# Long convolutions: one kind of PSUM bank for all steps, and filter columns loaded one at a time

## The chip, the cores and the metric

The kernel runs on one core of a Trainium2 chip. The metric is the device time of one execution in microseconds (us). A core has a matrix engine (TensorE, PE in the rows; its weight loads are PEld), a vector engine (VectorE, DVE), an activation engine (ScalarE, ACT), a general-purpose engine (GpSimd, POOL) and a sync engine (SyncE, SP) whose queue issues most of the transfers here. Each engine takes its instructions in order. Matmul results land in PSUM, which has eight banks of 128 partitions by 512 float32 each.

## The reference, cut to what matters

An encoder layer runs over two requests, of 256 and 2048 tokens. One projection of the normalised input feeds two mixers: gated long convolutions over 512 channels, and dilated window attention with 8 heads. Both results are normalised, concatenated, projected and added to the input; a gated feed-forward part follows. The mixer that the change touches:

```python
def long_conv(z, kf, skip):
    L = z.shape[1]
    zf = z.astype(jnp.float32)
    y = jnp.fft.irfft(jnp.fft.rfft(zf, n=2 * L, axis=1) * kf[None], n=2 * L, axis=1)[:, :L]
    return (y + skip.astype(jnp.float32) * zf).astype(z.dtype)

def hyena_mixer(u, short_w, short_b, w1, b1, sin_freq, w2, b2, w3, decay, skip):
    ...
    z = x1 * long_conv(v, kf[:, 0], skip[0])
    z = x2 * long_conv(z, kf[:, 1], skip[1])
    return z
...
    hy = hyena_mixer(proj[..., :3 * HY_WIDTH], ...)
    at = dilated_attention(proj[..., 3 * HY_WIDTH:])
    mix = jnp.concatenate([rmsnorm(hy, hy_out_g), rmsnorm(at, attn_out_g)], axis=-1) @ w_out
```

## The kernel before

The long convolution is a Fourier transform in two factors, done with matmuls. For each request (r = 0, 1) and each of the two convolutions in a row (o = 0, 1), `hyena` runs four kinds of step, and each writes one PSUM bank (128 x 512 float32):

- hs1 (`hyena_first`, L692 and L693): the first factor. VectorE and GpSimd split the input into a high and a low part, two matmuls add up in a bank, ScalarE or VectorE copies it out, and the result `hae` goes to DRAM (`d_hA`).
- hs2k and hs2z (`hyena_second`, L723 and L727): the second factor, of the filter's columns `hk` and of the input's `hx`, with the table `htab`. VectorE scales the filter's (L725) and multiplies the two as complex numbers (L731 to L734), and GpSimd adds (L735).
- hs3 (L741): back through the second factor, one group later; ScalarE copies it to `hbe` (L744), which goes to DRAM (`d_hB`).
- hs4 (`hyena`, L778): back through the first factor, from `hD`; VectorE multiplies it by the gate `hg` (L779). For o = 0 the result goes on to hs1; for o = 1 it is stored as the mixer's result `d_hy` (L785).

There are 72 product groups (hs2k, hs2z, hs3) and 36 hs4 steps of two matmuls each, of which the long request has 64 and 32. hs2k and hs2z share a tag with two banks; hs1, hs3 and hs4 share another with one. `hk` has one buffer that holds two groups' columns, `hx` and the other 128 x 2 x 512 tiles share a ring of four, and the gates have two.

`mixers` (L1043 and on) weaves streams of work in the order in which they are written: the convolution's steps (`units`) beside the second half of the input projection (`project`, matmuls named pj), and then beside attention, by the numbers in `RATES`:

```python
    RATES = dict(p1=42, f=90, ad=36, h1=135, p2=39, h2=90, at=440)
            x = min(live, key=lambda y: (y[2] + 0.5) / y[1])
```

That order is an input to a scheduler, which then orders each engine's instructions by when it reckons that operands and buffers are ready. So the order on an engine depends on how many buffers a tile has.

Attention works through 216 blocks of two heads. For each, TensorE computes scores (aS, L906 and L907), VectorE adds the bias and takes the minimum (L910) and ScalarE the exponential (L913) into `aP`, TensorE transposes this (aT, L922), VectorE or ScalarE copies it to `aPT`, and TensorE multiplies by the values (aOp, L938). The scores and the transposes have two banks each, the values' products one; with the convolution's three, all eight are in use.

After both mixers comes the output projection, in nine blocks of 256 tokens (matmuls named om, L208 to L210). Its first block is the short request; its merged rows are ready before attention ends. Every other block needs the long request's convolution (`ohy`, loaded from `d_hy` at L1124) and all three attention branches (`oO`, L1122).

Of the kernel before, what the change touches and what calls it, by code (L numbers as in the profile page):

```python
# [13 lines left out]
F32 = mybir.dt.float32  # L14
# [4 lines left out]
PSUM = bass.MemoryType.PSUM  # L19
DRAM = bass.MemoryType.DRAM  # L20

P = 128
# [3 lines left out]
C = 512  # L26
# [163 lines left out]
class Hybrid:  # L190
# [488 lines left out]
    def hyena_first(self, wp, psp, r, An, n, z):  # L679

        nc = self.nc
        f1 = self.hc[r][0]
        for k in range(2):
            S = self.ring(wp, "hS", F32R)
            for h in range(2):
                own, oth = slice(64 * h, 64 * h + 64), slice(64 - 64 * h, 128 - 64 * h)
                nc.vector.tensor_copy(S[own, h], z[own, k])
                self.sub(nc.gpsimd, S[oth, h], z[own, k], S[own, h])
            ae = self.ring(wp, "hae")
            for h in range(2):  # L690
                ps = psp.tile([P, C], F32, tag="hpt", name="hs1", bufs=1)
                nc.tensor.matmul(ps, f1[:, 0], S[:, h], start=True, stop=False)  # L692
                nc.tensor.matmul(ps, f1[:, 1], S[:, h], start=False, stop=True)  # L693
                (nc.vector.tensor_copy if h else nc.scalar.copy)(ae[:, h], ps)
            nc.sync.dma_start(out=An[n + k], in_=ae)
            yield

    def hyena_second(self, wp, psp, r, o, A, B):

        nc = self.nc  # L700
        n2c = REQ[r][1] // 64
        rnc = wp.tile([P, C], F32, tag="hrn", name="hrn", bufs=1)
        nc.sync.dma_start(out=rnc, in_=self.rnc[r][o][0].partition_broadcast(P))
        grp = "(g p) c -> p g c"
        Ag = A.rearrange("m n c -> (m n) c").rearrange(grp, p=P)
        Kg = self.fA[r][o].rearrange("m n c -> (m n) c").rearrange(grp, p=P)
        Bg = B.rearrange(grp, p=P)
        prev = None
        be = None
        for g in range(n2c + 1):  # L710
            cur = None
            if g < n2c:
                i = g % 2
                if i == 0:
                    gs = slice(g, g + 2)
                    tab = wp.tile([P, 2, 2, P], F32, tag="htab", name="htab", bufs=2)
                    nc.sync.dma_start(out=tab, in_=self.a[f"tab_{r}"][:, gs])
                    xz = self.ring(wp, "hx")
                    nc.sync.dma_start(out=xz, in_=Ag[:, gs])
                    xk = wp.tile([P, 2, C], F32, tag="hk", name="hk", bufs=1)  # L720
                    nc.sync.dma_start(out=xk, in_=Kg[:, gs])
                ps = psp.tile([P, C], F32, tag="hps", name="hs2k")
                nc.tensor.matmul(ps, tab[:, i, 0], xk[:, i], start=True, stop=True)  # L723
                K = wp.tile([P, C], F32, tag="hK", name="hK", bufs=2)
                nc.vector.tensor_tensor(out=K, in0=ps, in1=rnc, op=ALU.mult)  # L725
                ps = psp.tile([P, C], F32, tag="hps", name="hs2z")
                nc.tensor.matmul(ps, tab[:, i, 0], xz[:, i], start=True, stop=True)  # L727
                t1 = wp.tile([P, C], F32, tag="ht1", name="ht1", bufs=3)
                t2 = wp.tile([P, C], F32, tag="ht2", name="ht2", bufs=1)
                v, lo_, up = nc.vector, slice(0, 64), slice(64, 128)  # L730
                v.tensor_tensor(out=t1[lo_], in0=ps[lo_], in1=K[lo_], op=ALU.mult)  # L731
                v.tensor_tensor(out=t1[up], in0=ps[lo_], in1=K[up], op=ALU.mult)
                v.scalar_tensor_tensor(out=t2[lo_], in0=ps[up], scalar=-1.0, in1=K[up], op0=ALU.mult, op1=ALU.mult)
                v.tensor_tensor(out=t2[up], in0=ps[up], in1=K[lo_], op=ALU.mult)  # L734
                nc.gpsimd.tensor_tensor(out=t1, in0=t1, in1=t2, op=ALU.add)  # L735
                cur = (g, tab, t1)
                yield
            if prev is not None:
                g2, tb, pp = prev
                ps = psp.tile([P, C], F32, tag="hpt", name="hs3", bufs=1)  # L740
                nc.tensor.matmul(ps, tb[:, g2 % 2, 1], pp, start=True, stop=True)  # L741
                if g2 % 2 == 0:
                    be = self.ring(wp, "hbe")
                nc.scalar.copy(be[:, g2 % 2], ps)  # L744
                if g2 % 2 == 1:
                    nc.sync.dma_start(out=Bg[:, g2 - 1:g2 + 1], in_=be)
                yield
            prev = cur

    def hyena(self, wp, psp, r):  # L750

        nc = self.nc
# [15 lines left out]
        for o in range(2):  # L768
            yield from self.hyena_second(wp, psp, r, o, A[o], B[o])
            Bm = B[o].rearrange("(m h n) c -> n m h c", h=2, n=nh)  # L770
            for q0 in range(0, nh, 2):
                x = rows_in(self.tok["x2" if o else "x1"], q0, "hg")
                for k in range(2):
                    D = self.ring(wp, "hD")
                    nc.sync.dma_start(out=D, in_=Bm[q0 + k])
                    ps = psp.tile([P, C], F32, tag="hpt", name="hs4", bufs=1)
                    for h in range(2):
                        nc.tensor.matmul(ps[64 * h:64 * h + 64], gi, D[:, h], start=True, stop=True)  # L778
                    nc.vector.tensor_tensor(out=x[:, k], in0=ps, in1=x[:, k], op=ALU.mult)  # L779
                    yield  # L780
                if o == 0:
                    yield from self.hyena_first(wp, psp, r, An[1], q0, x)
                else:
                    for h, rows in enumerate(self.time_major(self.tok["hy"], r, q0)):
                        nc.sync.dma_start(out=rows, in_=x[64 * h:64 * h + 64])  # L785
# [88 lines left out]
    def attention(self, wp, psS, psT, psO, first, mq):  # L874
        nc, a = self.nc, self.a
        q1, q2 = [], []

        def scores(heads, g, i, blk, ot, bias, b):
# [2 lines left out]
            dil = DILS[b]  # L881
            off, L = REQ[r]
            ps = psS.tile([P, 2, 256], F32, tag="aS", name="aS")
            sb = wp.tile([P, 2, 256], F32, tag="aP", name="aP", bufs=3)
            for hh in range(2):
                Ql, Ks, Qh = heads[hh]
                t0 = off + res + dil * P * j
# [91 lines left out]
        for hp in range(4):  # L979
# [6 lines left out]
            for b in range(3):  # L986
# [6 lines left out]
                for g in self.attention_groups(b, (0, 1) if hp == 3 else (1, 0)):  # L993
# [3 lines left out]
                    for i, blk in enumerate(blks):  # L997
# [3 lines left out]
                        sb, n = scores(heads, g, i, blk, ot, bias, b)  # L1001
# [41 lines left out]
    def mixers(self):  # L1043
        R = self.RATES
        proj, first, atn, left, hy = (ExitStack() for _ in range(5))
        ps = self.pool(proj, "p_ps", bufs=2, space=PSUM, side="right")
        psF = self.pool(left, "f_ps", bufs=2, space=PSUM, side="left")
        hp = self.pool(proj, "p_h", side="right")
        wp = self.pool(proj, "p_w", side="right")
# [12 lines left out]
        g = self.project(hp, wp, w2, ps, range(0, 12), H)  # L1062
# [5 lines left out]
        hb = self.pool(hy, "h_c", side="left")  # L1068
        self.hyena_consts(hb)
        wh = self.pool(hy, "h_w", side="left")  # L1070
        psH = self.pool(hy, "h_ps", bufs=2, space=PSUM, side="left")

        def units():
            for r in range(2):
# [3 lines left out]
        with ExitStack() as st:  # L1078
# [8 lines left out]
            g = self.project(hp, wp, None, ps, range(12, 24))  # L1087
# [598 lines left out]
```

## Time and profile before

| | |
|---|---|
| median of three runs | 3568.52 us (3553.45 to 3568.69) |
| the profiled execution | 3565.03 us, its span 3562.9 us |
| TensorE busy | 3303.1 us, 93% of the span |
| VectorE / ScalarE / GpSimd busy | 69% / 44% / 35% |
| mean granted clock of TensorE in the record | 0.957 |
| moved by DMA | 628 MB, 176 GB/s over the span |

The profile is of one execution. Busy time of TensorE is modelled from pipelined matmuls and so can overlap: what a matmul costs in a dense stretch is the distance to the next one and not its duration. A 128 x 512 float32 matmul shows as two records. An engine's idle time is put down to what released it. In the clock row, 9 is the full 2.4 GHz.

### The profile page before, as it was taken

The page shows a single profiled execution, that of the slowest core. Times are in us where ns is not written, and L with a number is a line of the kernel's source. Part 1 is how long each engine was busy: PE and PEld are TensorE (multiplying, and loading weights), DVE is VectorE, ACT ScalarE, POOL GpSimd, SP SyncE. Part 2 cuts the span into 40 slices and gives each one's busy share as a digit, 9 for nine tenths or more (in the row PEclk, how much of TensorE's full clock was granted, in tenths as well). Part 3 has the DMA queues.
Part 4 walks back from the last instruction along what each step waited for, and adds up shares of the span by engine and source line. Part 5 has one row for each costly group of instructions (what it writes and reads, how often), then busy time and mean ns, then how long its engine had stood idle before and what let it go on. Part 6 is the DMA issues. An engine that isn't in the chain of part 4 may idle for free.

```text
span 3562.9 us, 56859 instructions
## 1 busy us (share of the span) xinstructions
PE 3303.1 (93%) x20926; PEld 3020.3 (85%) x20926; DVE 2465.5 (69%) x4254; ACT 1561.9 (44%) x2926; POOL 1255.2 (35%) x946
## 2 busy tenths in 40 slices
PE   7989899999899999996588799999899999899998
PEld 4978798889677788773388799999899999899998
DVE  7898877764576564686388666766776666567657
ACT  4577753323345565541255433333433334344433
POOL 1487751124222231222144433333634333223222
PEclk9999999999989999997699899999999999999999
DMA  6453567676756585656666632444544224466655
GB/s 240 134 179 122 154 186 240 225 223 199 202 173 194 149 235 157 187 176 195 212 188 199 198 108 106 153 154 151 218 147 150 95 94 147 155 205 217 221 179 181
DMA packets 408334, 628.02 MB, mean 176 GB/s; under 512 B 28431, under 2 KB 231439, under 8 KB 402135
## 3 DMA queue, kind: packets, MB, share of 16 engines
q1 hardware_dynamic: 354896, 593.13, 51.2%
q10 hardware_dynamic: 52072, 28.40, 2.7%
q8 instruction: 166, 2.72, 0.3%
q0 software_dynamic: 1088, 2.85, 0.2%
q14 instruction: 112, 0.92, 0.1%
HBM read 419.03 MB, written 205.25 MB: 175 GB/s over the span
## 4 chain that ended last, share of the span: by engine, by line
PE 58%; DVE 7%; DMA 7%; issue 2%; ACT 2%; SPq 1%; POOL 1%; ACTq 0%; DVEq 0%; POOLq 0%
PE w L210 8%; PE w L208 8%; PE w L209 8%; PE fd L210 4%; PE fd L209 4%; PE fd L208 4%; PE aOp L938 4%; PE aS L906 2%; PE aS L907 2%; PE aT L922 2%; PE hs2k L723 1%; PE hs2z L727 1%; PE hs L741 1%; PE pj L209 1%; PE pj L208 1%
## 5 line engine op out<-in xcount | busy, mean ns | idle before, releaser
L208 PE MATMUL w<-hh,whi 128*128 128x288 f32 (+1 forms) x2464 | 735.4, 299 | 16.3 <-ACT whi L1345 9.9
L210 PE MATMUL w<-hh,wlo 128*128 128x290 f32 (+1 forms) x2464 | 732.2, 298 | 10.7 <-POOL wlo L203 7.0
L209 PE MATMUL w<-hl,whi 128*128 128x288 f32 (+1 forms) x2464 | 735.2, 299 | 5.2 <-DVE hl L203 5.1
L208 PEld LDWEIGHTS w<-hh,whi 128*128 128x128 f32 x2464 | 470.3, 191 | 18.2 <-ACT whi L1345 10.1
L210 PEld LDWEIGHTS w<-hh,wlo 128*128 128x128 f32 x2464 | 469.4, 191 | 12.7 <-POOL wlo L203 8.0
L209 PEld LDWEIGHTS w<-hl,whi 128*128 128x128 f32 x2464 | 472.0, 192 | 6.7 <-DVE hl L203 6.6
L208 PE MATMUL pj<-hThi,wihi 128*128 128x386 f32 (+1 forms) x1152 | 402.5, 350 | 6.6 <-ACT u L629 4.1
L209 PE MATMUL pj<-hTlo,wihi 128*128 128x386 f32 (+1 forms) x1152 | 400.9, 348 | 7.8 <-DVE hTlo L203 7.8
L210 PE MATMUL pj<-hThi,wilo 128*128 128x386 f32 (+1 forms) x1152 | 397.8, 345 | 0.0
L208 PE MATMUL fd<-hh,dwh 128*128 128x288 f32 x1210 | 359.9, 297 | 12.6 <-ACT dwh L1551 12.6
L210 PE MATMUL fd<-hh,dwl 128*128 128x288 f32 x1210 | 358.8, 297 | 0.0
L209 PE MATMUL fd<-hl,dwh 128*128 128x288 f32 x1210 | 357.5, 295 | 0.0
L735 POOL TENSOR_TENSOR ht<-ht,ht 128x512 f32<-128x512 f32 x72 | 99.0, 1376 | 432.3 <-DVE ht L734 364.1
L208 PEld LDWEIGHTS fd<-hh,dwh 128*128 128x128 f32 x1210 | 229.8, 190 | 13.3 <-ACT dwh L1551 12.9
L209 PEld LDWEIGHTS pj<-hTlo,wihi 128*128 128x128 f32 x1152 | 221.8, 193 | 20.7 <-DVE hTlo L203 9.7
L938 PEld LDWEIGHTS aOp<-aV,aPT 128*128 128x128 f32 (+1 forms) x1408 | 193.9, 196 | 52.5 <-issue 20.3
L208 PEld LDWEIGHTS pj<-hThi,wihi 128*128 128x128 f32 x1152 | 221.1, 192 | 17.7 <-ACT u L629 4.4
L210 PEld LDWEIGHTS pj<-hThi,wilo 128*128 128x128 f32 x1152 | 220.9, 192 | 12.2 <-issue 8.0
L209 PEld LDWEIGHTS fd<-hl,dwh 128*128 128x128 f32 x1210 | 229.3, 190 | 0.4
L210 PEld LDWEIGHTS fd<-hh,dwl 128*128 128x128 f32 x1210 | 227.6, 188 | 0.1
L203 POOL TENSOR_TENSOR wlo<-ws,whi 128x512 fp32r<-128x512 f32 x88 | 133.4, 1516 | 235.9 <-ACT whi L1345 235.9
L910 DVE CUSTOM_DVE_ANT_0 aP<-aS,aB 128x256 f32<-128x256 f32 (+2 forms) x432 | 136.2, 355 | 115.6 <-PE aS L907 43.4
(297 smaller groups left out, 7977.3 us busy)
## 6 DMA issues: line engine op xcount, KB each, us to landing
hl<-d_G SPq DMA_DIRECT2D x154, 288.0 KB, 5.3
dwl<-d_S SPq DMA_DIRECT2D x59, 704.0 KB, 4.1
wiraw<-in_w_in SPq DMA_DIRECT2D x72, 512.0 KB, 4.6
d_G<-cv SPq DMA_DIRECT2D x42, 576.0 KB, 3.0
wraw<-in_w_gate SPq DMA_DIRECT2D x22, 1024.0 KB, 4.8
wraw<-in_w_up SPq DMA_DIRECT2D x22, 1024.0 KB, 5.6
adat<-in_ada_t SPq DMA_DIRECT2D x36, 512.0 KB, 4.6
d_fA<-fae SPq DMA_DIRECT2D x72, 256.0 KB, 3.1
```

Of the source, the lines that this page charges most:

```text
L203: eng.tensor_tensor(out=lo, in0=x, in1=hi.bitcast(F32), op=ALU.subtract)
L208: mm(out, wh, xh, start=first, stop=False, skip_group_check=more)
L209: mm(out, wh, xl, start=False, stop=False, skip_group_check=more)
L210: mm(out, wl, xh, start=False, stop=last, skip_group_check=more)
L723: nc.tensor.matmul(ps, tab[:, i, 0], xk[:, i], start=True, stop=True)
L727: nc.tensor.matmul(ps, tab[:, i, 0], xz[:, i], start=True, stop=True)
L735: nc.gpsimd.tensor_tensor(out=t1, in0=t1, in1=t2, op=ALU.add)
L906: nc.tensor.matmul(ps[:, hh, :N], qa, rhs, start=True, stop=False)
L907: nc.tensor.matmul(ps[:, hh, :N], qb, rhs, start=False, stop=True)
L910: nc.vector.tensor_tensor_reduce(out=sb[:, hh, :n], in0=ps[:, hh, v0:v0 + n], in1=bias[:, hh, b0:b0 + n], scale=1.0, scalar=3e38, op0=ALU. ...
L922: nc.tensor.transpose(pt[:cn, hh, c], sb[:, hh, c0:c0 + cn], self.ident)
L938: nc.tensor.matmul(po[:, i, hs], pe[:cn, hh, c], vt[:cn, x["v"] + c * x["vs"], hs], start=(c == 0), stop=(c == len(ch) - 1))
```

## The change

Three things change. The tags `hps` (two banks) and `hpt` (one bank) become one tag `hp` with three banks, for all steps of the convolution. The filter's columns are loaded one group at a time into three buffers of 128 x 512, and no longer two groups at a time into one buffer of 128 x 2 x 512. To make room for them, the attention's `aP` goes from three buffers to two.

```diff
--- before.py
+++ after.py
@@ -688,7 +688,7 @@
                 self.sub(nc.gpsimd, S[oth, h], z[own, k], S[own, h])
             ae = self.ring(wp, "hae")
             for h in range(2):
-                ps = psp.tile([P, C], F32, tag="hpt", name="hs1", bufs=1)
+                ps = psp.tile([P, C], F32, tag="hp", name="hs1")
                 nc.tensor.matmul(ps, f1[:, 0], S[:, h], start=True, stop=False)
                 nc.tensor.matmul(ps, f1[:, 1], S[:, h], start=False, stop=True)
                 (nc.vector.tensor_copy if h else nc.scalar.copy)(ae[:, h], ps)
@@ -717,13 +717,13 @@
                     nc.sync.dma_start(out=tab, in_=self.a[f"tab_{r}"][:, gs])
                     xz = self.ring(wp, "hx")
                     nc.sync.dma_start(out=xz, in_=Ag[:, gs])
-                    xk = wp.tile([P, 2, C], F32, tag="hk", name="hk", bufs=1)
-                    nc.sync.dma_start(out=xk, in_=Kg[:, gs])
-                ps = psp.tile([P, C], F32, tag="hps", name="hs2k")
-                nc.tensor.matmul(ps, tab[:, i, 0], xk[:, i], start=True, stop=True)
+                xk = wp.tile([P, C], F32, tag="hk", name="hk", bufs=3)
+                nc.sync.dma_start(out=xk, in_=Kg[:, g])
+                ps = psp.tile([P, C], F32, tag="hp", name="hs2k")
+                nc.tensor.matmul(ps, tab[:, i, 0], xk, start=True, stop=True)
                 K = wp.tile([P, C], F32, tag="hK", name="hK", bufs=2)
                 nc.vector.tensor_tensor(out=K, in0=ps, in1=rnc, op=ALU.mult)
-                ps = psp.tile([P, C], F32, tag="hps", name="hs2z")
+                ps = psp.tile([P, C], F32, tag="hp", name="hs2z")
                 nc.tensor.matmul(ps, tab[:, i, 0], xz[:, i], start=True, stop=True)
                 t1 = wp.tile([P, C], F32, tag="ht1", name="ht1", bufs=3)
                 t2 = wp.tile([P, C], F32, tag="ht2", name="ht2", bufs=1)
@@ -737,7 +737,7 @@
                 yield
             if prev is not None:
                 g2, tb, pp = prev
-                ps = psp.tile([P, C], F32, tag="hpt", name="hs3", bufs=1)
+                ps = psp.tile([P, C], F32, tag="hp", name="hs3")
                 nc.tensor.matmul(ps, tb[:, g2 % 2, 1], pp, start=True, stop=True)
                 if g2 % 2 == 0:
                     be = self.ring(wp, "hbe")
@@ -773,7 +773,7 @@
                 for k in range(2):
                     D = self.ring(wp, "hD")
                     nc.sync.dma_start(out=D, in_=Bm[q0 + k])
-                    ps = psp.tile([P, C], F32, tag="hpt", name="hs4", bufs=1)
+                    ps = psp.tile([P, C], F32, tag="hp", name="hs4")
                     for h in range(2):
                         nc.tensor.matmul(ps[64 * h:64 * h + 64], gi, D[:, h], start=True, stop=True)
                     nc.vector.tensor_tensor(out=x[:, k], in0=ps, in1=x[:, k], op=ALU.mult)
@@ -881,7 +881,7 @@
             dil = DILS[b]
             off, L = REQ[r]
             ps = psS.tile([P, 2, 256], F32, tag="aS", name="aS")
-            sb = wp.tile([P, 2, 256], F32, tag="aP", name="aP", bufs=3)
+            sb = wp.tile([P, 2, 256], F32, tag="aP", name="aP", bufs=2)
             for hh in range(2):
                 Ql, Ks, Qh = heads[hh]
                 t0 = off + res + dil * P * j
@@ -1068,7 +1068,7 @@
         hb = self.pool(hy, "h_c", side="left")
         self.hyena_consts(hb)
         wh = self.pool(hy, "h_w", side="left")
-        psH = self.pool(hy, "h_ps", bufs=2, space=PSUM, side="left")
+        psH = self.pool(hy, "h_ps", bufs=3, space=PSUM, side="left")
 
         def units():
             for r in range(2):
```

The instructions stay the same but for 36 more loads; their order on the engines changes. TensorE at the end of attention, before (L922 and L938 are attention, L723, L727 and L741 the convolution's products, L1174 the transposes that open the output projection):

```order
L938 MATMUL aOp<-aV,aPT 128x65 x4
L922 MATMUL aT<-ident,aP 128x128
L727 MATMUL hs2z<-hx,htab 128x512
L938 MATMUL aOp<-aV,aPT 128x65 x2
L741 MATMUL hs_12131<-ht_11943,htab 128x512
L723 MATMUL hs2k<-hk,htab 128x512
L1174 MATMUL ot<-ident,ohy 128x128 x4
L1174 MATMUL ot<-ident,oat 128x128 x4
L741 MATMUL hs_12255<-ht_12074,htab 128x512
L1174 MATMUL ot<-ident,ohy 128x128 x4
```

The same place now:

```order
L906 MATMUL aS<-Ks,Qh 128x256
L907 MATMUL aS<-Ks,Ql 128x256
L922 MATMUL aT<-ident,aP 128x128 x3
L938 MATMUL aOp<-aV,aPT 128x65 x4
L922 MATMUL aT<-ident,aP 128x128 x4
L938 MATMUL aOp<-aV,aPT 128x65 x4
L1174 MATMUL ot<-ident,ohy 128x128 x4
L1174 MATMUL ot<-ident,oat 128x128 x4
```

Before, products of the convolution stood among the last of attention and behind it; now there are none there. TensorE at the convolution's last hs4 steps (L778, in this view named hs), before:

```order
L778 MATMUL hs_14371<-hD,hgi_5119 64x512 x2
L778 MATMUL hs_14454<-hD,hgi_5119 64x512 x2
L778 MATMUL hs_14512<-hD,hgi_5119 64x512 x2
L1174 MATMUL ot<-ident,ohy 128x128 x4
L1174 MATMUL ot<-ident,oat 128x128 x4
```

And now:

```order
L922 MATMUL aT<-ident,aP 128x128 x4
L938 MATMUL aOp<-aV,aPT 128x65 x12
L778 MATMUL hs_14584<-hD,hgi_5119 64x512 x2
L922 MATMUL aT<-ident,aP 128x128
L922 MATMUL aT<-ident,aP 64x128
L906 MATMUL aS<-Ks,Qh 128x256
L907 MATMUL aS<-Ks,Ql 128x256
```

The last of them moved from right ahead of the second block's output transposes to between blocks of attention. On SyncE's queue, the convolution's last store (L785) and the load of its result (L1124), before:

```order
L763 DMA hg<-d_x_84 64x1024 x2
L785 DMA d_hy<-hg 64x1024 x4
L1124 DMA ohy<-d_hy 128x512 x2
L1122 DMA oO<-d_O_89 128x528
L1122 DMA oO<-d_O_90 128x528
```

And now, where L958 are the last stores of attention:

```order
L958 DMA d_O_91<-aO 128x3x132
L958 DMA d_O_91<-aO 128x132
L1124 DMA ohy<-d_hy 128x512
L1192 DMA mg<-in_mixg 128x1024
L1197 DMA oraw<-in_w_out 128x8x128 x2
L1122 DMA oO<-d_O_91 128x528 x2
L1124 DMA ohy<-d_hy 128x512
```

The load of `ohy` now stands behind attention's last stores, and no longer behind the convolution's.

## Rows read from the trace of the kernel before

**Rows 1.** The page: busy time, and the clock in 40 slices.
```profile
PE 3303.1 (93%) x20926; PEld 3020.3 (85%) x20926; DVE 2465.5 (69%) x4254; ACT 1561.9 (44%) x2926; POOL 1255.2 (35%) x946
...
PEclk9999999999989999997699899999999999999999
```

**Rows 2.** Stages: from:to, length, busy us of each engine (instructions), clock, DMA share, GB/s.
```profile
500.00:944.00 444.00, 415.13 (x2182) 382.78 (x2181) 281.83 (x392) 140.79 (x220) 101.25 (x61) 0.97 0.69 218
944.00:1592.80 648.80, 623.21 (x3401) 499.54 (x3400) 430.98 (x1355) 345.75 (x830) 167.82 (x128) 0.96 0.62 184
1592.80:1754.30 161.50, 96.77 (x355) 46.20 (x354) 76.41 (x123) 25.35 (x47) 27.92 (x23) 0.69 0.69 217
1754.30:1990.30 236.00, 213.40 (x1664) 207.85 (x1662) 187.94 (x381) 128.45 (x273) 98.44 (x93) 0.94 0.61 185
```

**Rows 3.** Chain that ended last, in attention: start, us, what.
```profile
1399.61 1.01 PE hs L778 x4
...
1446.10 0.86 PE hs2z L727 x2
```

**Rows 4.** Timeline behind attention: start, us, engine, line, what, idle time before it.
```profile
1697.85 0.69 DVE L779 TENSOR_TENSOR hg<-hs,hg 128x512 f32<-128x512 f32 x1 [5.47 <-DMA hg<-d_x]
...
1701.37 1.98 PE L778 MATMUL hs<-hD,hgi 128*64 128x512 f32 x4 [0.80 <-DVE hg L779]
...
1705.75 0.69 DVE L779 TENSOR_TENSOR hg<-hs,hg 128x512 f32<-128x512 f32 x1 [4.43 <-DMA hg<-d_x]
```

**Rows 5.** Waits of SyncE's queue, 944 to 1750: us in total, times, longest.
```profile
SPq L763 <- DMA d_hy<-hg: 20.8, 6, 3.8
```

**Rows 6.** 1592.8 to 1749, busy PE and PEld, of L723, L727, L741 and L778 in turn.
```profile
1592.80:1749.00 156.20, 12.11 (x20) 3.74 (x20) 0.70 0.69 217
...
1592.80:1749.00 156.20, 11.46 (x20) 3.30 (x20) 0.70 0.69 217
...
1592.80:1749.00 156.20, 14.61 (x24) 4.08 (x24) 0.70 0.69 217
...
1592.80:1749.00 156.20, 31.59 (x64) 4.76 (x64) 0.70 0.69 217
```

**Rows 7.** Timeline from the end of attention to the second output block.
```profile
1592.25 0.56 PE L938 MATMUL aOp<-aV,aPT 128*128 128x65 f32 x4
...
1600.47 0.48 PE L208 MATMUL om<-omh,ow 128*128 128x256 f32 x2
...
1745.38 0.63 ACT L1147 ACTIVATE oO<-ohy 128x512 f32<-128x512 f32 x1 [71.08 <-DMA ohy<-d_hy]
...
1754.34 1.01 PE L208 MATMUL om<-omh,ow 128*128 128x256 f32 x3
```

**Rows 8.** Instructions of `om`: ns min/median/max, first and last start.
```profile
L210 PE MATMUL om<-omh,owl x360: 277/283/562, 1636.6 to 1990.0; 128*128 128x256 f32 x180
```

**Rows 9.** Lines of PE, 944 to 1592.8: busy us, mean ns, idle before and releasers.
```profile
L906 PE MATMUL aS<-Ks,Qh 128*128 128x256 f32 (+1 forms) x432 | 188.6, 443 | 3.6 <-DVE aO L910 3.6
...
L727 PE MATMUL hs2z<-hx,htab 128*128 128x512 f32 x100 | 57.4, 658 | 7.4 <-DVE ht L734 6.8 <-DMA hx<-d_hA 0.5
L741 PE MATMUL hs<-ht,htab 128*128 128x512 f32 x99 | 55.2, 640 | 4.8 <-POOL ht L735 4.8
L723 PE MATMUL hs2k<-hk,htab 128*128 128x512 f32 x98 | 53.2, 625 | 5.4 <-DMA hk<-d_fA 3.6 <-DVE Ks L871 1.3 <-DVE hK L725 0.5
```

**Rows 10.** Instructions of `aP`: ns min/median/max, first and last start.
```profile
L910 DVE CUSTOM_DVE_ANT_0 aP<-aS,aB x432: 274/353/426, 954.9 to 1587.8; 128x256 f32<-128x256 f32 x58, 128x128 f32<-128x128 f32 x53, 128x192 f32<-128x192 f32 x33
L913 ACT ACTIVATE aP<-aP,aO x432: 384/455/524, 955.5 to 1588.3; 128x256 f32<-128x256 f32 x58, 128x128 f32<-128x128 f32 x53, 128x192 f32<-128x192 f32 x33
```

**Rows 11.** DMA issues: count, KB each, median us to landing.
```profile
hk<-d_fA SPq DMA_DIRECT2D x36, 512.0 KB, 4.2
...
hg<-d_x SPq DMA_DIRECT2D x36, 256.0 KB, 3.6
```

## The prediction

> **What bounds the kernel now.** I read the busy line and the slices first, then the granted clock by stage, then the chain of waits and the timeline where the clock is low. TensorE is busy for 93% of the span and its clock is granted in full nearly everywhere, except in two or three slices in the middle [rows 1]. Cut into stages, the picture is plain [rows 2]: the second half of the projection (500 to 944 us) and attention (944 to 1592.8) keep TensorE busy 415 of 444 and 623 of 649 us at a clock of 0.96 to 0.97; the stretch from the last attention matmul to the output projection of its second block (1592.8 to 1754.3) is 161.5 us long, TensorE is busy there for 97 us and the clock is 0.69. That stretch is the end of the long convolution standing alone. Beside one block of the output projection, it has nothing else to run, because the second block waits for `ohy`, the convolution's last result: ScalarE's first square of it comes after an idle time of 71 us that ends with that load, at 1745 [rows 7].
>
> Inside the stretch the inverse step (L778, called hs4 in the kernel) is the slowest part. Two steps form a pair, and pairs come every 7.9 us (1697.85 to 1705.75) [rows 4]. The step has one PSUM bank, so a matmul group waits until VectorE has multiplied the previous one; VectorE in turn waits 5.47 and 4.43 us for the `hg` load; the load waits for the store from the same pair of buffers, 20.8 us in six waits [rows 5]. TensorE runs at its lower level there, 1.2 GHz: four records of L778 take 1.98 us against 1.01 us in attention at 2.4 GHz [rows 3, 4].
>
> **What the change does to the order.** The change has three edits, but the larger effect is that the scheduler now lets the convolution run ahead. In the order of TensorE's instructions, 13 of the 72 hs2k matmuls stand ahead of the first attention score before, 30 after; behind the last attention matmul stood 10 hs2k, 10 hs2z, 12 hs3 and 32 hs4 matmuls, and now none does. The trace shows the same count for the tail: 20, 20, 24 and 64 records, two for a matmul [rows 6]. The last hs4 group now stands 29 blocks of attention before its end. The sum is therefore about a serial stretch that goes, and work that reappears where TensorE is already the bound.
>
> **The sum**, against the profiled execution (3565.0 us; its span is 3562.9). It is 3.5 us under the median of the runs shown, less than these differ among themselves (3553 to 3569), so I make no correction.
>
> 1. Removed: the whole stretch, 161.5 us [rows 2].
> 2. The same matmuls, at full clock, in the projection and attention. hs2k, hs2z and hs3: (10 + 10 + 12) x 0.86 = 27.5 us; hs4: 16 steps x 1.01 = 16.2 us [rows 3, 6]. Together 43.7 us. TensorE idles 29 + 26 us in these two stages [rows 2]; if it all filled such holes the term would be 0, if none it is 43.7. I take 43.7, as these holes are waits for data and not a want of work. It falls on the projection: 17 hs2k, 17 hs2z and 16 hs3 move there (50 x 0.86 = 43 us), while attention loses 7 hs2k, 7 hs2z and 4 hs3 (15.5 us) and gains 16 hs4 steps (16.2 us), so keeps its length.
> 3. What must still lie between attention's last matmul and the second output block. Before, the first output matmul came 7.7 us after that last group (1592.8 to 1600.47); this stays [rows 7]. Then the first block's output projection, which the convolution's tail hid and which is now exposed. Blocks two to nine run from 1754.3 to 1990 [rows 2, 8], so one takes 236 / 8 = 29.5 us. I take that value: 37.2 us in all. The ends: TensorE's busy time alone, 213.4 / 8 = 26.7 us (34 in all), and 9 us more if the second block comes late by the whole way from its `ohy` to its first matmul (1745.4 to 1754.3; 46 in all). The second block's rows of the last attention branch are loaded just behind the last store, as before; its `ohy` is in DRAM by then.
> 4. The convolution's steps wait inside attention: 7.4 + 4.8 + 5.4 = 17.6 us for about 50 steps of the second kind, 0.35 us a step [rows 9]. For the 11 steps moved in from the tail: 4 us (ends: 0, and 17.6 for all 50 that wait again).
> 5. The score buffer `aP` goes from three to two. A softmax (L910, 432 of them, two for a block, so 216 blocks) can now write only after the transposes of the block two before. In the new order these transposes stand right behind the block's own scores, and what releases them, an exponential of two blocks ago, is long done. The trace of before shows TensorE waiting 3.6 us in all for VectorE ahead of scores [rows 9]; I add as much again, 4 us. The lower end is -4 (nothing excludes a gain from a tighter order), the upper one is in the rivals.
> 6. The filter load: 36 loads of 512 KB become 72 of 256 KB, one buffer becomes three of half the size. TensorE waited 3.6 us for `hk` in attention [rows 9]; at most that goes, and I count 0. The 36 further issues lie on SP's queue beside transfers that land in 3.6 to 4.2 us [rows 11]; a step is 3 x 0.86 = 2.6 us of TensorE, and three buffers let a load start up to two steps, 5.2 us, ahead even without attention between. With one step of cover, each would wait 3.6 - 2.6 = 1.0 us, 72 us in all at the worst.
> 7. One kind of bank for all steps: hs2k and hs2z shared two banks, hs1, hs3 and hs4 had one. Three in rotation give the product steps no more than they had, and the others up to three. The serial cost of the single bank, 1.98 + 0.8 us for each hs4 group [rows 4], goes with the stretch of term 1 and isn't counted twice.
>
> 3565.0 - 161.5 + 43.7 + 37.2 + 4 + 4 = 3492.4, say 3492 us.
>
> The 512 KB load of `hk` lands in 4.2 us and a 256 KB load in 3.6 [rows 11], so halving the size saves little and the transfers cost more in total. The Trainium skill says why one should not split: on its page "DMA: Bandwidth & Descriptors", section "Anatomy of one DMA — SWDGE (gpsimd) path", a transfer costs a fixed 2.0 us or so, whatever its size. By that rule alone, as an estimate, 36 more transfers add 72 us of transfer time, and the sum would be 3564 if it were all exposed; by the waits of the trace, it is hidden.
>
> **The rivals.**
>
> *The denser stages don't take the work for free (13%).* VectorE is busy 282 of 444 us in the projection and 431 of 649 in attention [rows 2], and each product step is five VectorE instructions, in order among attention's. For this speaks that TensorE's queue is in order as well, so a late product holds attention's scores. Against it: 50 such steps cost 17.6 us before. If each of the 216 blocks loses 0.2 us, 43 us come on top: 3535.
>
> *More is won (9%).* The waits of before in both stages (29 + 26 us) partly go with the rotation and the earlier loads, which can fill holes in front of scores and projections alike; against it, the rows that name them are mostly waits for VectorE and GpSimd, not for a bank [rows 9]. Half of the idle: 27 us, and 3 for the first output block at its lower end: 3462.
>
> *Slower: two score buffers tie attention to the softmax (4%).* If in each block one vector step of the softmax (0.353 us) and one exponential (0.455) stand in TensorE's way [rows 10], that is 0.81 x 216 = 175 us in place of 4: 3663. It decides from (3565 - 3492) / 216 = 0.34 us a block. Against it: TensorE is the slower partner (649 us for 216 blocks is 3.0 us a block, the softmax of a block 2 x 0.81 = 1.6), and the transposes stand early in the new order.
>
> *The order changes but the chip doesn't follow (2%).* The hs4 pairs now stand within some 26 blocks; if a pair still takes 7.9 us through its two `hg` buffers, and every one holds up attention for it, 8 x 7.9 = 63 us come back: 3555. Against it: 26 blocks are about 78 us of attention, which is longer than 63.
>
> *The clock falls with the rotating banks (2%).* A matmul group that waits a moment for its bank, step after step, might bring TensorE to the lower level in the middle of attention. The moved 43.7 us would then take as much again: 3536. With two banks going round in the same way the granted clock was 0.97 and 0.96 [rows 2], which speaks against it. The Trainium skill reports such a case in "TensorE: Matmul & The Clock Gate", section "A second HAM failure mode: psum-queue depth-cycling"; by that page the rival would hold, by these rows it doesn't.
>
> **How the numbers follow.** The forecast of 3492 has 70%; its own range, from the ends of terms 3 to 5 and a part of the idle time in term 2, is 3468 to 3515. A measurement of this kernel tells about 0.5% from no change, 18 us, so faster means under 3550.7. The forecast and the rivals at 3535, 3462 and 3536 are faster together, 94%; some 2% of the first rival's spread lies above 3550, so 92% remain. No change: the rival at 3555 and that spread, 4%. Slower: 4%. For 8 in 10 the range must hold the forecast and most of the two neighbours: 3455 to 3545.
>
> **What would show it.** In the new profile no L778 lies behind the last L938; the low digits of the clock row in the middle are gone but for one slice at most; attention starts some 43 us later and is 640 to 660 us long; between its last matmul and the second block's first L208 lie 34 to 46 us; L723 waits for `hk` no more than before. It would be wrong if attention grew by over 30 us with waits for VectorE or ScalarE ahead of L906 or L922, if L778 in attention waited for `hg` or `hD`, or if the output stage, now without its hidden first block, ran slower than 29.5 us a block.

## The result and the profile after

The changed kernel takes 3516.6 us (median of 4 runs, 3504.0 to 3517.8) and the one before 3567.0 (4 runs, 3553.5 to 3568.7): a ratio of 0.9859, 95% interval 0.9826 to 0.9892. It is 50 us faster; the forecast of 3492 was 75 under the same median. The profiled execution took 3504.0 us, the fastest of the four; its span is 3502.1.

The page's busy line and clock row, against [rows 1]:

```profile
PE 3290.7 (94%) x20926; PEld 3020.3 (86%) x20926; DVE 2461.5 (70%) x4254; ACT 1560.1 (45%) x2922; POOL 1267.1 (36%) x946
...
PEclk9999999999999999998999899999999999999999
```

The run of low digits (7 6 9 9 7) is gone; two single eights are left. The stages, against [rows 2], in the same columns (from:to, length, busy us of PE, PEld, DVE, ACT and POOL, clock, DMA share, GB/s): the second half of the projection, attention, and the output projection:

```profile
500.00:990.00 490.00, 460.95 (x2289) 399.31 (x2287) 344.86 (x475) 150.57 (x237) 123.49 (x78) 0.98 0.71 229
990.00:1655.90 665.90, 632.37 (x3428) 500.08 (x3426) 415.60 (x1343) 346.51 (x826) 161.28 (x123) 0.96 0.67 195
...
1655.90:1924.60 268.70, 236.85 (x1887) 231.86 (x1888) 212.27 (x434) 141.35 (x304) 124.04 (x105) 0.95 0.66 199
```

The projection grew from 444 to 490 us, since products of the convolution moved there, attention from 648.8 to 665.9. From attention's last matmul to the last output matmul it is 268.7 us, where it was 161.5 + 236 = 397.5.

The last steps of the convolution and of attention (median ns, first and last start; the inverse step hs4 is L778, `hs` in the trace):

```profile
L778 PE MATMUL hs<-hD,hgi x144: 592/604/1116, 616.9 to 1583.4; 128*64 128x512 f32 x144
```

```profile
L938 PE MATMUL aOp<-aV,aPT x1408: 218/275/477, 1003.7 to 1655.4; 128*128 128x65 f32 x152, 64*128 64x65 f32 x24
```

The last hs4 starts 72 us ahead of attention's last matmul. Before, it started at 1737.1, 144 us behind it [rows 2], and the matmuls counted in [rows 6] stood there.

Where attention ends, TensorE's timeline now has a hole of another kind ([rows 7] show this place before; start, us, what, and in brackets the idle time before it and its releaser):

```profile
1667.33 0.28 PE L210 MATMUL om<-omh,ow 128*128 128x256 f32 x1
1683.71 1.09 PE L1174 MATMUL ot<-ident,ohy 128*128 128x128 f32 x4 [16.11 <-DVE ohy L1159]
...
1686.36 0.58 PE L208 MATMUL om<-omh,ow 128*128 128x256 f32 x1 [0.70 <-DVE ox L1214]
1686.74 0.41 PE L209 MATMUL om<-oml,ow 128*128 128x256 f32 x1
...
1694.62 0.28 PE L208 MATMUL om<-omh,ow 128*128 128x256 f32 x1
```

The first output block stops after 48 matmuls, two banks' worth, for 16 us. TensorE stands at the second block's transposes, which wait for the normalised `ohy`; right behind them the first block goes on, and its matmuls wait for `ox` (L1214). TensorE's clock falls from 2.4 to 1.2 GHz in this idle time: the granted clock is 1.00 from 1663 to 1667.5 us and 0.51 from 1684 to 1690, and the same matmul is 0.28 us long ahead of it and 0.41 behind it. The row at 1694.62 is the second block's first L208 (the 25th on `ow`, of which a block has 24), 39 us behind attention. What stands behind the hole is seen on SyncE's queue (start, us, what it issued):

```profile
1666.89 8.20 SPq L1197 DMA_DIRECT2D oraw<-in_w_out  x3
1679.28 2.76 SPq L1207 DMA_DIRECT2D ox<-in_xD  x2
```

The weights `oraw` and the residual `ox` share a tag with two buffers. The first block's `ox` waits until weights have gone through those buffers, to 1679, and both banks of `om` are full until it is there; so the second block's transposes were put ahead. e5 below tests this. Before, the convolution's tail ran beside it. The first block's `ox` was late there too: VectorE's first use of it ended a wait for that load at 1627, 27 us behind the first output matmul [rows 7]:

```profile
1627.31 0.48 DVE L1214 SCALAR_TENSOR_TENSOR ox<-om,mod,ox 128x256 f32<-128x256 f32 x1 [1.39 <-DMA ox<-in_xD]
```

In attention the score buffer shows. The first row is the idle time of engines ahead of operations on `aP` until the transposes, before (us, times); the second is VectorE's longest wait of the list for 990 to 1655.9 now (us in total, times, longest); the next ones are TensorE's lines there:

```profile
  PE aT L922: 9.7, 13
```

```profile
DVE aP L910 <- PE aT L922: 79.4, 53, 4.8
```

```profile
L938 PE MATMUL aOp<-aV,aPT 128*128 128x65 f32 (+1 forms) x1408 | 213.1, 285 | 11.3 <-ACT aO L942 3.8 <-ACT aPT L926 3.3 <-DVE aPT L929 2.1
L906 PE MATMUL aS<-Ks,Qh 128*128 128x256 f32 (+1 forms) x432 | 187.5, 440 | 5.9 <-DVE aO L910 5.9
...
L922 PE MATMUL aT<-ident,aP 128*128 128x128 f32 (+1 forms) x704 | 130.3, 286 | 4.9 <-ACT aP L913 4.9
L741 PE MATMUL hs<-ht,htab 128*128 128x512 f32 x88 | 48.3, 632 | 3.1 <-POOL ht L735 1.5 <-DMA htab<-in_tab 0.8 <-DMA hk<-d_fA 0.7
L727 PE MATMUL hs2z<-hx,htab 128*128 128x512 f32 x86 | 48.0, 641 | 3.8 <-DMA hx<-d_hA 3.7
L723 PE MATMUL hs2k<-hk,htab 128*128 128x512 f32 x86 | 46.2, 620 | 0.8 <-DMA htab<-in_tab 0.8
```

So the wait for the transposes grew from 9.7 to 79.4 us. The wait of L723 for `hk`, 3.6 us in [rows 9], is gone.

### The profile page after: what moved, and what is told of

Its sections match the earlier page's. It is cut to its first block, busy times and chain, and to the rows that moved or that the text cites. A ratio compares the mean times of both kernels' runs of the same rounds, so it can differ in the third digit from the quotient of the medians.

```text
span 3502.1 us, 56839 instructions
## 1 busy us (share of the span) xinstructions
PE 3290.7 (94%) x20926; PEld 3020.3 (86%) x20926; DVE 2461.5 (70%) x4254; ACT 1560.1 (45%) x2922; POOL 1267.1 (36%) x946
## 4 chain that ended last, share of the span: by engine, by line
PE 42%; DVE 5%; DMA 2%; issue 2%; ACT 1%; POOL 1%; ACTq 0%; SPq 0%; DVEq 0%; POOLq 0%
PE w L210 9%; PE w L208 9%; PE w L209 9%; PE fd L210 4%; PE fd L209 4%; PE fd L208 4%; DVE fT L1251 1%; DMA hl<-d_opT 0%; DMA d_x1T<-ox 0%; DVE ohy L1159 0%; DVE ox L1214 0%; DVE hl L203 0%; POOL oat L1145 0%; PE om L208 0%; PE om L210 0%
## 5 line engine op out<-in xcount | busy, mean ns | idle before, releaser
L208 PE MATMUL w<-hh,whi 128*128 128x288 f32 (+1 forms) x2464 | 737.3, 300 | 13.1 <-ACT whi L1345 8.3
L208 PEld LDWEIGHTS w<-hh,whi 128*128 128x128 f32 x2464 | 472.2, 192 | 14.9 <-ACT whi L1345 8.6
L208 PE MATMUL pj<-hThi,wihi 128*128 128x386 f32 (+1 forms) x1152 | 403.4, 351 | 12.6 <-ACT u L629 5.2
L208 PE MATMUL fd<-hh,dwh 128*128 128x288 f32 x1210 | 360.4, 298 | 12.6 <-ACT dwh L1551 12.6
L938 PEld LDWEIGHTS aOp<-aV,aPT 128*128 128x128 f32 (+1 forms) x1408 | 197.1, 199 | 57.8 <-issue 18.4
L208 PEld LDWEIGHTS pj<-hThi,wihi 128*128 128x128 f32 x1152 | 221.3, 192 | 28.0 <-issue 7.8
L208 PEld LDWEIGHTS fd<-hh,dwh 128*128 128x128 f32 x1210 | 230.2, 190 | 13.3 <-ACT dwh L1551 12.8
L938 PE MATMUL aOp<-aV,aPT 128*128 128x65 f32 (+1 forms) x1408 | 213.1, 285 | 11.3 <-ACT aO L942 3.8
L910 DVE CUSTOM_DVE_ANT_0 aP<-aS,aB 128x256 f32<-128x256 f32 (+2 forms) x432 | 135.9, 354 | 120.7 <-PE aT L922 79.4
```

The lines of the kernel that those rows point to most:

```text
L208: mm(out, wh, xh, start=first, stop=False, skip_group_check=more)
L910: nc.vector.tensor_tensor_reduce(out=sb[:, hh, :n], in0=ps[:, hh, v0:v0 + n], in1=bias[:, hh, b0:b0 + n], scale=1.0, scalar=3e38, op0=ALU. ...
L938: nc.tensor.matmul(po[:, i, hs], pe[:cn, hh, c], vt[:cn, x["v"] + c * x["vs"], hs], start=(c == 0), stop=(c == len(ch) - 1))
```

## The experiments

Medians; a ratio is against the kernel before, on the same chip. The kernel before took 3563.1 us beside e1 to e4, 3565.6 beside e5 to e8, 3559.6 beside e9 to e11. "Attention" is the time from the first score's start (L906) to the start of the last value product (L938), "output" from there to the last output matmul's.

| run | hp banks | aP | hk | us, ratio (interval) | attention | output |
|---|---|---|---|---|---|---|
| before | 2 + 1 | 3 | pair | 3567.0 | 648 | 398 |
| changed | 3 | 2 | 3 single | 3516.6, 0.986 (0.983 to 0.989) | 665 | 269 |
| e4 changed, again | 3 | 2 | 3 single | 3513.6, 0.986 (0.984 to 0.988) | 668 | 275 |
| e1 | 3 | 3 | pair | 3490.5, 0.979 (0.977 to 0.981) | 655 | 275 |
| e2 | 2 + 1 | 2 | pair | 3556.5, 0.998 (0.996 to 0.999) | 706 | 334 |
| e3 | 3 | 2 | pair | 3504.8, 0.984 (0.982 to 0.985) | 671 | 270 |
| e9 as e3 | 3 | 2 | pair | 3504.1, 0.983 (0.981 to 0.985) | 676 | 273 |
| e6 | 3 | 3 | 2 single | 3486.3, 0.978 (0.976 to 0.980) | 654 | 275 |
| e10 | 3 | 2 | 2 single | 3506.9, 0.984 (0.982 to 0.986) | 678 | 270 |
| e7 | 1 + 2 | 3 | pair | 3623.0, 1.016 (1.015 to 1.017) | 629 | 471 |
| e8 | 2 + 1, other kinds | 3 | pair | 3494.6, 0.979 (0.978 to 0.981) | 645 | 289 |
| e5 | 3, early x | 3 | pair | 3480.5, 0.976 (0.975 to 0.977) | 645 | 268 |
| e11 | 3, early x | 2 | 3 single | 3513.8, 0.986 (0.983 to 0.988) | 667 | 268 |

The theory: the banks bring all of the gain, by taking the convolution's end into attention; aP's two buffers and the split load give some of it back. The rival: each part brings some.

**e1, the banks alone.** Of the change only the tag `hp` with three banks:

```diff
-psH = self.pool(hy, "h_ps", bufs=2, space=PSUM, side="left")
+psH = self.pool(hy, "h_ps", bufs=3, space=PSUM, side="left")
-ps = psp.tile([P, C], F32, tag="hpt", name="hs4", bufs=1)
+ps = psp.tile([P, C], F32, tag="hp", name="hs4")
...
```

> Only the banks: one tag with three banks for all steps; hk and aP as before. Theory (the banks let the convolution run ahead; the second aP buffer is given up at a cost): no convolution step behind attention, the whole gain of the change and some 15 us more, because attention keeps its three aP buffers: 3495 to 3510 us, attention some 650 us long. Rival (the longer attention comes from the convolution's last steps that now lie in it, not from aP): the same time as the changed kernel, 3510 to 3520, attention some 665 us long. Rival (the filter's single buffers are needed for the convolution to keep up): 3525 or more, with waits for hk ahead of L723.

3490.5 us, 73 less than before and 23 less than the full change beside it (e4). That is 4.5 us under the expected range. The banks bring more than the whole gain, and the two other edits cost. L778 of e1 ends inside attention too (last start 1624.0, last L938 1643.1).

**e2, aP's two buffers alone.**

```diff
-sb = wp.tile([P, 2, 256], F32, tag="aP", name="aP", bufs=3)
+sb = wp.tile([P, 2, 256], F32, tag="aP", name="aP", bufs=2)
```

> Only aP: two buffers in place of three; banks and hk as before. In the order, the product steps end inside attention, but all 16 hs4 steps of the last convolution stand behind it. Theory: the hs4 tail with its one bank stays, 16 steps at 7.9 us a pair, some 65 to 75 us behind attention; attention takes in 11 product steps (29 us) and loses some 15 us to waits for transposes: 3530 to 3560 us. Rival (aP costs nothing, and holding back attention is what helps): 3515 or less.

7 us faster, as expected. By itself it also moves work into attention: that is 57 us longer (44 were expected), and output 64 shorter. The convolution still runs behind attention, longer than expected: its last hs4 starts 87 us behind. There TensorE's longest wait is the gate (us, times, longest; 1652 to 1745):

```profile
PE hs L778 <- DVE hg L779: 29.0, 8, 13.7
```

**e3 and e9, banks and aP.** The same line edited on top of e1; e9 repeats e3 on another chip.

> Banks and aP as changed, hk as before. Against the banks alone it isolates aP, against the full change it isolates hk. Theory (hk hidden, aP dear): the time of the full change, 3510 to 3520, some 15 us over the banks alone. Rival (aP free): as the banks alone.

> Banks and aP without the hk edit, once more: its first runs were 3504 to 3509, 9 us under the full change. If that difference is real, 3503 to 3509 again; if it came with a better granted clock in attention, 3508 to 3518, as the full change.

3504.8 and 3504.1: aP costs 14 us over e1. The granted clock of the whole execution doesn't account for them: at a mean of 0.970, e1 took 3490.5 us, e3 3505.4 and e9 3504.1. For e3 the expectation was missed from below: 9 us remain to the full change beside it (e4), at the same clock (0.967 to 0.970 in e3, 0.966 to 0.971 in e4), so the split load with three buffers isn't free there; e9 confirmed the time of e3. VectorE's idle time ahead of the aP tile's operations, until the transposes, in e1 and then in e3:

```profile
  PE aT L922: 12.1, 13
```

```profile
  PE aT L922: 66.1, 50
```

Attention is 15 us longer in e3 than in e1, 21 in e9. Little of it is idle time of TensorE, which is idle in attention for 32 us in e1 and 33 in e3. The value products take longer there (e1, then e3), and the transposes 131.2 us in place of 127.0:

```profile
L938 PE MATMUL aOp<-aV,aPT 128*128 128x65 f32 (+1 forms) x1408 | 207.4, 280 | 2.3 <-ACT aO L942 1.2 <-DVE aPT L926 0.6 <-ACT aPT L926 0.5
```

```profile
L938 PE MATMUL aOp<-aV,aPT 128*128 128x65 f32 (+1 forms) x1408 | 215.3, 287 | 6.2 <-ACT aPT L926 3.3 <-DVE aPT L926 1.2 <-ACT aO L942 1.1
```

The mean clock of attention was 0.96 in e1, 0.95 in e3 and 0.93 in e9, so a part of these lengths is the clock; how much wasn't separated. A second pair differs in aP alone: e6 and e10 below, on two chips. The ratios are 0.978 and 0.984, their intervals lie apart, and the difference is worth 21 us. In their profiles attention has the same clock, 0.96, and is 23 us longer with two buffers; TensorE is idle there for 45 us in place of 29, most of the rise ahead of the value products (e6, then e10):

```profile
L938 PE MATMUL aOp<-aV,aPT 128*128 128x65 f32 (+1 forms) x1408 | 210.1, 283 | 7.8 <-ACT aPT L926 4.2 <-DVE aPT L926 2.5 <-ACT aO L942 1.0
```

```profile
L938 PE MATMUL aOp<-aV,aPT 128*128 128x65 f32 (+1 forms) x1408 | 210.4, 281 | 18.4 <-ACT aPT L926 9.5 <-ACT aO L942 5.6 <-DVE aPT L926 2.3
```

That giving up the third aP buffer costs 14 to 21 us is thus shown; by which wait it does so differs between the pairs and stays open.

**e4, the change again**, beside e1 to e3, unedited.

> The changed kernel itself, beside the three others on the same chip: 3504 to 3518 as before. Its profile shows whether the 13 us between its fastest run and the others lie in one stage.

3513.6: the first measurement repeats. The 9 us between the two profiles don't lie in one stage: output is 5 us longer in e4, and the projection and attention 2 each.

**e5, banks and an early x.** On top of e1 the weights leave the tag that they share with `ox`:

```diff
-raw = wp.tile([P, 8, 256], F32, tag="ox", name="oraw", bufs=2)[:, :, :P]
+raw = (self.rowp if m % 2 else wp).tile([P, 8, P], F32, tag="oraw", name="oraw", bufs=1)
```

> The banks alone, and the output projection's first block gets its x at once: the weights w_out 3 to 7 are loaded through two buffers of their own and no longer through the two that also hold x. In the profile with the banks alone, TensorE stands still for 17.6 us ahead of the second block's transposes, with only a quarter of the first block done. Theory (the first block is held back by its x, which comes behind the weights): in the order 160 of its 192 matmuls now lie ahead of these transposes; 14 us of TensorE work moves into the hole: 3475 to 3484 us. Rival (the later blocks are bound by VectorE and the transfers anyway): 3486 to 3494, no change against the banks alone.

3480.5, the best version, 10 us under e1 and 6 under e6, which ran on the same chip. TensorE's waits from the end of attention on, e1 (1643 to 1945) and then e5 (1631.5 to 1920):

```profile
PE ot L1174 <- DVE ohy L1159: 18.2, 3, 17.6
PE ot L1174 <- DVE oml L203: 15.7, 12, 1.9
```

```profile
PE ot L1174 <- DVE oml L203: 13.0, 6, 6.6
...
PE om L208 <- DVE ox L1214: 4.8, 4, 2.0
PE ot L1174 <- DVE ohy L1159: 2.5, 2, 1.4
```

The 18 us are gone, and output is 8 us shorter. The profiles differ by 10 us more in attention, which this edit can't explain; see the last section.

**e6, banks and the load one by one**, in two buffers, with aP at three (two single buffers take the room of the one pair):

```diff
-xk = wp.tile([P, 2, C], F32, tag="hk", name="hk", bufs=1)
-nc.sync.dma_start(out=xk, in_=Kg[:, gs])
+xk = wp.tile([P, C], F32, tag="hk", name="hk", bufs=2)
+nc.sync.dma_start(out=xk, in_=Kg[:, g])
```

> The banks, and the filter's columns one by one in two buffers (the same space as before, so aP keeps three). Isolates the one-by-one load. Theory (the load is hidden either way; the 9 us between the change and the same without its hk edit come from the order at the output stage): 3486 to 3497, as the banks alone, with no more waits for hk ahead of L723. Rival (36 more transfers cost some 9 us by themselves): 3497 to 3505, with waits for hk or longer landings.

3486.3 against 3490.5: the same within the intervals, if not a gain. TensorE's longest wait in e1 and then in e6, from 900 us to the end of attention:

```profile
PE hs2k L723 <- DMA hk<-d_fA: 9.0, 6, 2.8
```

```profile
PE hs2z L727 <- DMA hx<-d_hA: 11.5, 5, 5.1
```

The wait for `hk` goes and one for `hx` grows by 8 us in its place (3.6 in e1). The two medians are from two chips.

**e10, the full change with two buffers of hk** in place of three.

> The full change, but two buffers for the single filter columns in place of three. Theory (the one-by-one load costs nothing, as with the banks alone): as the banks with two aP buffers, 3503 to 3515 us. Rival (one-by-one loads cost some 9 us beside two aP buffers): 3512 to 3520.

3506.9 against e9's 3504.1: the split load with two buffers costs nothing clear of noise there either. The third buffer goes with some 7 us (to e4 and e11, at 3514), but e4 is from another chip and e11 has two more edits, the intervals overlap, and the clock was not the same: 0.972 to 0.973 in e10, 0.966 to 0.971 in e4. Within e11 the executions at 0.971 and 0.974 took 3504 and 3502 us, those at 0.966 to 0.968 3514 to 3516. So the 7 us may be the clock's as well as the buffer's. No wait for `hk` accounts for them: TensorE waits for it for 0.7 us in the change and 0.6 in e4. In the profiles the stretch behind the output projection is 1577 us long in the change and in e4, 1569 and 1570 in e9 and e10; but e11, also with three, has 1573, and e5, with the pair, 1576. The cause stays open.

**e7, two banks for the inverse kinds, one for the products.** With bufs=2 for hs1, hs3 and hs4 (tag `hpt`) and bufs=1 for hs2k and hs2z: three banks as before, dealt the other way.

> Three banks as before but the other way round: two for hs1, hs3 and hs4, one for hs2k and hs2z. Tests whether the single bank of hs4 is what held the convolution back, or the division itself. In the order, even more product steps lie behind attention (17 and 19, and all 16 hs4). Theory (the free choice among three is what counts; the products need two as much): a tail of some 190 us, 3570 to 3600 us; within it hs4 pairs come faster than 7.9 us, some 6.5 us. Rival (the second bank for hs4 is the gain): 3530 or less.

3623.0, slower than before, and by more than expected. The last hs4 starts 222 us behind attention (1807.8 against 1585.6), and there TensorE waits for the products of the step before (1585 to 1830; us, times, longest):

```profile
PE hs2k L723 <- DVE ht L734: 41.8, 13, 6.3
PE hs L778 <- DVE hg L779: 23.8, 5, 8.1
```

Among the last hs4 steps the pairs come every 7.0 us (1776.3 to 1804.5, four pairs), 7.9 before. So a second bank for hs4 makes these steps a little faster, but it is not what helps if the products pay for it.

**e8, hs3 with a bank of its own.** hs1 and hs4 move to the products' pair:

```diff
-ps = psp.tile([P, C], F32, tag="hpt", name="hs4", bufs=1)
+ps = psp.tile([P, C], F32, tag="hps", name="hs4")
```

> hs1 and hs4 share the two banks of the products; hs3 keeps one alone. In the order, 6 of the 16 last hs4 steps lie behind attention. Theory (the tail costs by what lies in it): 6 steps at 7.9 us a pair, some 24 us, less what the first output block covers: 3495 to 3512 us, between the banks alone and before. Rival (hs3 alone in its bank holds all groups back): 3540 or more.

3494.6, as good as e1 within the intervals and 0.4 us under the expected range, though two kinds of bank remain and six hs4 steps still run behind attention:

```profile
L778 PE MATMUL hs<-hD,hgi x144: 592/643/1117, 621.8 to 1660.6; 128*64 128x512 f32 x144
```

The last starts at 1660.6, 25 us behind attention's last matmul (1635.5) and so within the first output block. So that all kinds go round isn't needed; it is enough that hs3 doesn't share a single bank with hs1 and hs4. Which of these two it has to be parted from wasn't tried.

**e11, the full change with an early x** (the edit of e5, and one buffer of `osq` in place of two, to make room).

> The full change, with the output projection's first x loaded at once (the weights through two buffers of their own, one buffer less for the squares). Theory (the 16 us hole ahead of the second block's transposes, 139 of 192 matmuls moved in front of it): 8 to 12 us under the full change, 3502 to 3508; three aP buffers would still be better (3480 with the banks alone and this edit). Rival (the hole moves on to the next wait): 3511 to 3520.

3513.8 against e4's 3513.6 and the change's 3516.6: no gain in the median, and the expectation was missed. With the spread of e11 by the clock (see e10) a gain of some us can't be excluded. The hole is gone, but other waits stand there: the list of e11 for 1661 to 1940 begins (behind these stand 4.1 us for `omh` and 3.4 for `ox`)

```profile
PE w L208 <- ACT whi L1345: 8.6, 1, 8.6
PE ot L1174 <- DVE ohy L1159: 5.2, 4, 2.2
PE ot L1174 <- DVE oml L203: 5.2, 5, 2.7
```

and output takes 267.5 us against 269.3 (the change) and 274.7 (e4). What differs from e5 besides aP and hk is `osq`; which of them eats the gain wasn't tried.

## Why the prediction was right, and where its sizes were off

The mechanism held: the end of the convolution leaves the serial stretch and fits into the stages ahead. The range for 8 in 10 (3455 to 3545) held the time; the forecast's own range (3468 to 3515) missed it by 1.6 us. 25 us of the expected gain are missing, half of them in the profile, half because the profiled execution was the fastest of four. Of the 12 us in the profile, 3 lie in the projection, 8 in attention and 5 behind the output projection, where no edit reaches and the profiles of this case differ by as much as 13; the output part gave back 4.5.

1. *The removed stretch and the moved work (terms 1 and 2)* are right. Attention starts 46 us later (944 to 990), where 43 were forecast for the 50 products; attention with three aP buffers keeps its length (645 to 655 us in e1, e5, e6 and e8, against 648).
2. *The exposed first block (term 3)* is right in size: 39 us to the second block, 37.2 forecast, and the whole output part 269 against 236 + 37 = 273. Its making was not foreseen, so that the size came out is in part luck: 16 us of it are the hole that comes with the late `ox`, and the first block's last matmuls run into the second block. From there, blocks two to nine take (1924.7 - 1694.6) / 8 = 28.8 us each.
3. *aP's two buffers (term 5)* is the step that was mis-sized. I let only a wait of TensorE count and took 4 us, from "what releases them ... is long done"; e1 to e3 is 14 us and e6 to e10 21, and attention in the six profiles with three shared banks and two aP buffers is 665 to 678 us, in those of e1, e5, e6 and e8 645 to 655. The sign of 640 to 660 us failed for the changed kernel (666). VectorE's wait for the transposes, 9.7 us before, is 79 us in the change and 66 in e3. The rival in which this ties attention has the right place, but at 14 / 216 = 0.065 us a block (0.10 by e6 to e10) it is far from the 0.34 from which it decides.
4. *Convolution steps in attention (term 4)* was counted with the wrong sign: it charges 4 us there for 11 steps, while term 2 has attention lose product steps. Ahead of L741, L727 and L723 TensorE now waits 3.1 + 3.8 + 0.8 = 7.7 us, 17.6 before. L778 waits 2.6 us for `hD` there and not for `hg`.
5. *The split load (term 6)* counted 0. With two buffers it is that within the noise (e6, e10); in the full change, with three, 9 us go with it (e3 to e4), waits for `hk` aren't the reason, and the cause stays open. The Trainium skill's page "DMA: Bandwidth & Descriptors", section "Anatomy of one DMA — SWDGE (gpsimd) path", has a fixed 2.0 us a transfer; by that, 36 more would cost an estimated 72 us if exposed. They are not: e6 is no slower than e1. That section is about transfers that GpSimd issues, and these are on SyncE's queue. The prediction's guess that halving a load saves little is borne out: `hk` lands in 5.5 us as a pair in e1 and in 5.0 us as single columns in e6.
6. *One kind of bank (term 7)* shows no cost in e1, and e7 and e8 sharpen it: it matters which steps share.

3492 + 10 (aP, 14 in place of 4) + 9 (the load with three buffers) = 3511, within 6 of the median; both corrections are read from the runs, so this is no test of the sum. The test is e1: without terms 5 and 6 the forecast is 3488, and e1 is 2 us off it.

The rival of a falling clock isn't borne out: with three banks in rotation it is granted at 0.98 in the projection and 0.96 in attention. The case that the Trainium skill reports in "TensorE: Matmul & The Clock Gate", section "A second HAM failure mode: psum-queue depth-cycling", for a bf16 kernel, doesn't occur here. That the denser stages cost 43 us isn't borne out either: e1, which has them without the other two edits, is 2 us from a sum that charges nothing for them.

## What to carry to other kernels

Where step kinds of a pipeline have PSUM banks of their own, look for the kind that waits on a single one; sharing all banks lets the order run ahead, and so can a better split (e8), while a worse one cost 57 us (e7). Count what pays for the room: here three edits came together, and the banks alone are 23 us faster than all three. When a tail that hid something goes, look at what stood beside it: the first output block's x was late all along and showed only then.

## What was not expected of the hardware

e1 and e5 have the same order of TensorE's instructions up to the output projection, and yet attention takes 655.3 us in one and 644.9 in the other. The granted clock differs (columns as in the stages above; 987 to 1430 us in three pieces, e1 and then e5):

```profile
987.00:1130.00 143.00, 130.93 (x699) 101.76 (x699) 95.09 (x279) 76.23 (x171) 43.25 (x32) 0.95 0.70 202
1130.00:1280.00 150.00, 142.94 (x833) 116.18 (x834) 87.00 (x302) 82.39 (x198) 51.97 (x39) 0.93 0.69 200
1280.00:1430.00 150.00, 141.47 (x743) 109.96 (x743) 108.70 (x308) 77.13 (x180) 34.85 (x27) 0.97 0.66 191
```

```profile
987.00:1130.00 143.00, 132.70 (x720) 104.10 (x719) 99.20 (x289) 78.78 (x177) 41.34 (x32) 0.97 0.73 210
1130.00:1280.00 150.00, 144.38 (x862) 120.25 (x862) 88.85 (x311) 84.47 (x203) 51.83 (x39) 0.97 0.70 205
1280.00:1430.00 150.00, 141.74 (x742) 108.47 (x742) 111.67 (x313) 78.73 (x181) 36.14 (x28) 0.99 0.64 184
```

In the middle piece TensorE is as busy in both (143 and 144 of 150 us), at 0.93 and 0.97 of 2.4 GHz, and 833 or 862 matmul records stand in it. One profile's stage is thus uncertain by some 10 us here, as much as the smaller effects above; these rest on medians.

The time in which a load lands doesn't follow from its size alone: `hk` took 4.2 us for 512 KB before [rows 11] and 5.5 in e1, where it isn't edited, and 5.2 us for 256 KB in the change; `hg`, not edited, took 3.6 us [rows 11] and then 6.1 (e1's row first, then the change's):

```profile
hk<-d_fA SPq DMA_DIRECT2D x36, 512.0 KB, 5.5
```

```profile
hk<-d_fA SPq DMA_DIRECT2D x72, 256.0 KB, 5.2
...
hg<-d_x SPq DMA_DIRECT2D x36, 256.0 KB, 6.1
```
